# Weight casts of more than 512 columns, issued as two casts of 512

## The chip, the cores and the metric

The kernel runs on one core of a Trainium2 chip. A core has several engines that run side by side, each through a queue of its own: TensorE (PE in the profile; its weight loads are PEld), VectorE (DVE), ScalarE (ACT), GpSimd (POOL), and SyncE (SP), which here issues the transfers. The metric is the device time of one execution in microseconds (us).

## The reference

The reference is a decoder trunk of two layers over 512 tokens with 1024 features, in float32. Each layer adds to the residual stream half of a SwiGLU feed-forward block, then a mixer, then half of a second feed-forward block, each behind an RMS norm; the first mixer is a chunked gated linear attention, the second a stick-breaking attention. A final RMS norm ends it.

```python
def swiglu(h, w_gate, w_up, w_down):
    return (jax.nn.silu(h @ w_gate) * (h @ w_up)) @ w_down
...
for i in range(DEPTH):
    x = x + 0.5 * swiglu(rmsnorm(x, ffn1_norm[i]), ffn1_w_gate[i], ffn1_w_up[i], ffn1_w_down[i])
    h = rmsnorm(x, mix_norm[i])
    ...
    x = x + y.astype(x.dtype)
    x = x + 0.5 * swiglu(rmsnorm(x, ffn2_norm[i]), ffn2_w_gate[i], ffn2_w_up[i], ffn2_w_down[i])
return rmsnorm(x, final_norm)
```

The hidden width of a feed-forward block is 2816, so the four blocks hold most of the weights and of the products.

## The kernel before, in words

Activations lie feature by feature: eight tiles of 128 features by 512 tokens. Every float32 operand of a large product is split into a high part, which is the value cast to the type that TensorE takes (F32R), and a low part, which is the value minus the high part. A product of two such operands is three products on TensorE: high by high, low by high, high by low.

For the weights this split is made on the chip. A `Chunk` is one transfer of weights into a raw tile; an `Entry` is a step of work, which consists of one to four weight units and a body that issues TensorE's products. `Entry.split` takes each unit, casts it on ScalarE into the high tile `wh` (L138) and subtracts on VectorE to get the low tile `wl` (L139). Most units are 128 partitions by 1024 columns; some are 512. Where a unit comes as a tuple of two pieces, each piece of 512 columns has its own cast and subtraction. The large `wh` and `wl` tiles rotate through four buffers each, so a cast must wait until TensorE has finished with the unit that had its buffer before; units of fewer than 1024 columns have one buffer.

`Feed` holds the entries in the order of the program. `Feed.start` issues the splits of up to three entries ahead (at most four large units), the views of four and the transfers of six, and then starts the entry's body. So the casts for a later entry are written ahead of the products and evacuations of the present one. Within each engine the order of the queue is laid out when the program is built, from the written order and from what would be ready; TensorE's order in most of the feed-forward phases is the written one, by `tc.issue_after(st["pe"])`.

Most of the gate and up products and a third of the down products use a scheme of seven block products in place of eight (`FFN.seven`, `seven_down`). Its weight units are a quarter of the weights, sums of quarters that VectorE makes (`sums_12`, L694 and L695; `sums_34`, L700 and L701; L368 to L376 for the down weights), and the other quarters. Each sum tile is written by two VectorE instructions of 512 columns. The seven products run as body_1 and body_2:

```python
prod(w, a11, 0, half(0, 0))
nc.scalar.copy(z, w)
yield
prod(q, s, 0, lambda j: self.t_half(0, j))
nc.scalar.copy(pair(o1[:, H:T]), flat(q))
yield
prod(w, s, 4, lambda j: self.t_half(1, j), first=False)
```

`nc.scalar.copy(z, w)` is L736: ScalarE copies the first accumulator `ps_w` into `ps_z`, after which the third product adds to `ps_w`. The products are L709. ScalarE also evacuates accumulators (L739, L742, L754) and applies the gate's activation (L719); VectorE adds (L722, L755, L759). `seven_down` has the same pattern (products L384, copy L402, additions L390).

The first three entries are split by hand in `begin` and do not pass through L138.

Of the kernel before, what the change touches and what calls it, by code (L numbers as in the profile page):

```python
# [46 lines left out]
def decoder(ctx: ExitStack, tc: tile.TileContext, a: dict, out: bass.AP):  # L47
    nc = tc.nc
# [59 lines left out]
    class Entry:  # L108
# [13 lines left out]
        def split(self):  # L122
            if self.W is None:
                self.W = []
                for r, (_, _, n, m) in zip(self.view(), self.units):
                    few = n * m < 1024
                    if few:

                        h, l = (
                            st["few"].tile([P, n * m], F32R, tag="v" + t, bufs=1, name="w" + t) for t in "hl"  # L130
                        )
                    else:
                        h, l = (wp.tile([P, n * m], F32R, tag="w" + t, bufs=4, name="w" + t) for t in "hl")
                    h, l = (t.rearrange("p (n m) -> p n m", m=m) for t in (h, l))
                    pieces = r if isinstance(r, tuple) else (r,)
                    for i, part in enumerate(pieces):
                        k = slice(i * n // len(pieces), (i + 1) * n // len(pieces))
                        st["cut"] = nc.scalar.copy(h[:, k], part).ins  # L138
                        nc.vector.tensor_tensor(out=l[:, k], in0=part, in1=h[:, k].bitcast(F32), op=ALU.subtract)  # L139
                    self.W.append((h, l))  # L140

# [335 lines left out]
    st = {}  # L477
# [1427 lines left out]
```

## Time and profile before

| what | value |
|---|---|
| time, median of 3 runs (lowest to highest) | 1781.22 us (1780.61 to 1783.96) |
| span of the profiled execution | 1780.3 us |
| PE, PEld busy | 1760.9, 1632.9 us |
| DVE busy | 1538.8 us |
| ACT busy | 1050.4 us, 1830 instructions |
| transfers | 179.24 MB, 101 GB/s in the mean |

The profiled execution is given by its span, from the first to the last instruction; the page shows no time around it. The engine rows give the time in which an engine ran at least one instruction, with the share of the span and the number of instructions. A group of instructions is written as line, engine, operation, output tile and input tile, shapes and count; after the bar come its busy time and the mean duration of one in ns, then the idle time of the engine just before such instructions and what ended it. A wait is written as engine, waiting tile and line, `<-`, engine, tile and line of what released it, then us in total, number of times and, in most rows, the longest. The chain is the work that ended last, followed back from the end: each piece has its start, its length and what ran. The mean granted clock of TensorE was 0.999 of full speed.

### The profile page before, as it was taken

How to read it: one execution, taken by the hardware profiler on the slowest of the kernel's cores; microseconds unless marked ns; L12 is line 12 of the kernel's file. 1: busy time of each engine (PE TensorE's matmuls, PEld its weight loads, DVE VectorE, ACT ScalarE, POOL GpSimd, SP SyncE). 2: the span in 40 equal slices, each digit the busy share in tenths (PEclk: the TensorE clock that was granted, in tenths of full speed). 3: DMA queues.
4: the chain of work that ended last, by engine and by line, in shares of the span. 5: the costliest groups of instructions: out<-in, count | busy, mean ns of one | idle time of the engine just before them, and what ended most of it. 6: DMA issues, size and time to landing. Idle time of an engine off the chain costs nothing.

```text
span 1780.3 us, 31182 instructions
## 1 busy us (share of the span) xinstructions
PE 1760.9 (99%) x12714; PEld 1632.9 (92%) x12714; DVE 1538.8 (86%) x2527; ACT 1050.4 (59%) x1830; POOL 9.8 (1%) x24
## 2 busy tenths in 40 slices
PE   9999999999999999999999999999999999999998
PEld 8999999889888899999889999999888888999997
DVE  8999797786878999889798988977898679998986
ACT  7556455554655556555555555655888755565554
POOL 0000000100000000000000000000000000000000
PEclk9999999999999999999999999999999999999999
DMA  5433334322122333333323233322212233333331
GB/s 167 142 115 112 107 97 131 93 72 72 49 95 95 106 108 119 107 107 108 114 88 119 96 119 104 122 84 83 83 48 72 71 95 119 111 103 111 104 125 53
DMA packets 178755, 179.24 MB, mean 101 GB/s; under 512 B 4082, under 2 KB 170276, under 8 KB 178612
## 3 DMA queue, kind: packets, MB, share of 16 engines
q1 hardware_dynamic: 177760, 175.91, 31.5%
q8 instruction: 99, 1.62, 0.4%
q0 software_dynamic: 608, 1.05, 0.2%
q14 instruction: 44, 0.36, 0.1%
q10 hardware_dynamic: 244, 0.29, 0.0%
HBM read 175.17 MB, written 2.10 MB: 100 GB/s over the span
## 4 chain that ended last, share of the span: by engine, by line
PE 62%; DVE 26%; ACT 7%; issue 3%; DMA 1%; DVEq 0%; ACTq 0%; SPq 0%
PE ps_w L709 13%; PE ps_d L80 12%; PE ps_f L80 8%; DVE wl L139 8%; PE ps_q L709 6%; PE ps_t L80 5%; PE ps_z L709 3%; PE ps_b L80 3%; ACT wh L138 3%; PE ps_w L384 2%; DVE x L390 2%; PE ps_z L1394 1%; DVE ts L816 1%; DVE xn L800 1%; DVE nl L807 1%
## 5 line engine op out<-in xcount | busy, mean ns | idle before, releaser
L139 DVE TENSOR_TENSOR wl<-raw,wh 128x1024 fp32r<-128x1024 f32 x241 | 254.9, 1058 | 58.4 <-ACT wh L138 57.7
L138 ACT CAST wh<-raw 128x1024 fp32r<-128x1024 f32 x241 | 221.7, 920 | 72.7 <-PE ps_f L80 21.6
L139 DVE TENSOR_TENSOR wl<-s,wh 128x1024 fp32r<-128x1024 f32 x176 | 214.3, 1218 | 42.2 <-ACT wh L138 41.9
L138 ACT CAST wh<-s 128x1024 fp32r<-128x1024 f32 x176 | 184.3, 1047 | 102.1 <-DVE s L701 25.7
L709 PE MATMUL ps_w<-th,wh 128*128 128x256 f32 x864 | 239.9, 278 | 4.5 <-ACT ps_z L736 3.4
L709 PE MATMUL ps_w<-tl,wh 128*128 128x256 f32 x864 | 237.7, 275 | 0.0
L709 PE MATMUL ps_w<-th,wl 128*128 128x256 f32 x864 | 237.7, 275 | 0.0
L709 PEld LDWEIGHTS ps_w<-th,wh 128*128 128x128 f32 x864 | 165.8, 192 | 8.2 <-ACT ps_z L736 7.9
L80 PE MATMUL ps_f<-xh,wh 128*128 128x512 f32 x432 | 166.1, 385 | 1.1 <-DVE x L260 1.1
L709 PEld LDWEIGHTS ps_w<-tl,wh 128*128 128x128 f32 x864 | 165.9, 192 | 0.0
L709 PEld LDWEIGHTS ps_w<-th,wl 128*128 128x128 f32 x864 | 165.9, 192 | 0.0
L80 PE MATMUL ps_f<-xh,wl 128*128 128x512 f32 x432 | 164.2, 380 | 0.5 <-DVE wl L139 0.5
L80 PE MATMUL ps_f<-xl,wh 128*128 128x512 f32 x432 | 164.0, 380 | 0.0
L80 PE MATMUL ps_d<-hl,wh 128*128 128x512 f32 x416 | 158.0, 380 | 0.9 <-DVE hl L807 0.8
L80 PE MATMUL ps_d<-hh,wh 128*128 128x512 f32 x416 | 157.7, 380 | 0.2 <-ACT hh L806 0.2
L80 PE MATMUL ps_d<-hh,wl 128*128 128x512 f32 x416 | 157.7, 379 | 0.0
L138 ACT CAST wh<-rawd 128x1024 fp32r<-128x1024 f32 (+1 forms) x100 | 82.7, 844 | 61.2 <-PE ps_d L80 44.5
L139 DVE TENSOR_TENSOR wl<-rawd,wh 128x1024 fp32r<-128x1024 f32 (+1 forms) x100 | 95.9, 962 | 15.3 <-ACT wh L138 15.2
L80 PEld LDWEIGHTS ps_f<-xh,wh 128*128 128x128 f32 x432 | 81.7, 189 | 12.5 <-DVE x L260 1.5
L80 PEld LDWEIGHTS ps_f<-xl,wh 128*128 128x128 f32 x432 | 81.7, 189 | 11.5
L80 PEld LDWEIGHTS ps_f<-xh,wl 128*128 128x128 f32 x432 | 81.7, 189 | 11.4 <-DVE wl L139 0.9
L339 DVE SCALAR_TENSOR_TENSOR x<-ps_d,x 128x512 f32<-128x512 f32 x120 | 79.9, 682 | 13.7 <-PE ps_d L80 13.5
(352 smaller groups left out, 5245.8 us busy)
## 6 DMA issues: line engine op xcount, KB each, us to landing
raw<-in_ffn_w_gate_dram SPq DMA_DIRECT2D x43, 1024.0 KB, 5.4
raw<-in_ffn_w_up_dram SPq DMA_DIRECT2D x43, 1024.0 KB, 5.4
rawd<-in_ffn_w_down_dram SPq DMA_DIRECT2D x84, 512.0 KB, 3.7
raw<-in_gla_w_in_dram SPq DMA_DIRECT2D x12, 1024.0 KB, 5.3
raw<-in_sb_w_in_dram SPq DMA_DIRECT2D x16, 512.0 KB, 3.7
raw<-in_gla_w_out_dram SPq DMA_DIRECT2D x4, 1024.0 KB, 5.0
raw<-in_sb_w_in_dram SPq DMA_DIRECT2D x4, 1024.0 KB, 5.1
raw<-in_sb_w_out_dram SPq DMA_DIRECT2D x4, 1024.0 KB, 4.9
```

Of the source, the lines that this page charges most:

```text
L80: st["pe"] = nc.tensor.matmul(ps, l, r, start=first, stop=last).ins
L138: st["cut"] = nc.scalar.copy(h[:, k], part).ins
L139: nc.vector.tensor_tensor(out=l[:, k], in0=part, in1=h[:, k].bitcast(F32), op=ALU.subtract)
L339: nc.vector.scalar_tensor_tensor(out=x, in0=flat(ps), scalar=0.5, in1=x, op0=ALU.mult, op1=ALU.add)
L384: st["pe"] = nc.tensor.matmul(ps, l_, r_, start=first and c + n == 0, stop=c == 1 and n == 2, skip_group_check=True).ins
L390: nc.vector.scalar_tensor_tensor(out=x, in0=ps, scalar=0.5, in1=x, op0=ALU.mult, op1=ALU.add)
L709: st["pe"] = nc.tensor.matmul(o, l_, r_, start=first and j + n == 0, stop=j == 3 and n == 2, skip_group_check=True).ins
L800: nc.vector.scalar_tensor_tensor(out=t, in0=xs[k], scalar=g, in1=st["R"], op0=ALU.mult, op1=ALU.mult)
L807: nc.vector.tensor_tensor(out=l, in0=t, in1=h.bitcast(F32), op=ALU.subtract)
L816: nc.vector.tensor_tensor(out=o, in0=p, in1=q, op=ALU.subtract)
L1394: nc.tensor.matmul(o_, l_, r_, start=first, stop=last, skip_group_check=True)
```

## The change

The cast of a piece at L138 is issued in steps of `512 // m` rows of the unit, where `m` is the length of a row. A unit of 8 x 128, 4 x 256 or 2 x 512 columns gets two casts of 512 columns; a piece of 512 columns or fewer still gets one. The subtraction stays one instruction over the whole piece. The result of the cast is no longer kept in `st["cut"]`.

```diff
                         k = slice(i * n // len(pieces), (i + 1) * n // len(pieces))
-                        st["cut"] = nc.scalar.copy(h[:, k], part).ins
+                        rows = k.stop - k.start
+                        step = max(1, min(rows, 512 // m))
+                        for a0 in range(0, rows, step):
+                            nc.scalar.copy(h[:, k.start + a0 : k.start + a0 + step], part[:, a0 : a0 + step])
                         nc.vector.tensor_tensor(out=l[:, k], in0=part, in1=h[:, k].bitcast(F32), op=ALU.subtract)
```

## The prediction

> **What bounds the kernel now.** I read the page's sums first, then its chain, then the busy time by stage, and then the waits that end at the operations around the casts.
>
> ```profile
> span 1780.3 us, 31182 instructions
> PE 1760.9 (99%) x12714; PEld 1632.9 (92%) x12714; DVE 1538.8 (86%) x2527; ACT 1050.4 (59%) x1830; POOL 9.8 (1%) x24
> ...
> PE 62%; DVE 26%; ACT 7%; issue 3%; DMA 1%; DVEq 0%; ACTq 0%; SPq 0%
> ```
>
> TensorE is busy for 99% of the span, so no more than 1780.3 - 1760.9 = 19.4 us of it are open gaps. The chain all the same leaves TensorE for 38% of its length: VectorE and ScalarE run beside it with hardly any spare time, and the chain changes over to them wherever TensorE waited a little. The sums by stage show where:
>
> ```profile
> 20.00:70.00 50.00, 49.43 (x250) 42.37 (x249) 49.32 (x79) 28.20 (x45) 0.00 (x0) 1.00 0.37 117
> 100.00:150.00 50.00, 49.86 (x422) 48.84 (x422) 47.72 (x81) 28.37 (x51) 0.00 (x0) 1.00 0.31 96
> 1550.00:1600.00 50.00, 49.77 (x441) 49.29 (x441) 49.27 (x81) 30.85 (x58) 0.00 (x0) 1.00 0.34 106
> 1600.00:1650.00 50.00, 49.95 (x381) 47.83 (x380) 41.55 (x69) 25.98 (x46) 0.00 (x0) 1.00 0.37 116
> ```
>
> After the length of the stretch come the busy times of PE, PEld, DVE and ACT. In the feed-forward phases VectorE is busy for 41.6 to 49.3 of 50 us while TensorE never falls under 49.4; ScalarE stays at 26 to 31. ScalarE is not short of time, but it works strictly in its queue's order, and some of what it does is waited for at once. One piece of the chain, from just before a TensorE gap, shows that:
>
> ```profile
> 150.50 0.35 DVE o L755
> 150.85 0.02 issue
> 150.87 0.42 ACT o L719
> 151.29 0.94 ACT wh L138
> 152.22 0.58 ACT o L719 x2
> 152.81 0.94 ACT wh L138
> 153.75 0.28 ACT ps_z L736
> 154.03 0.04 issue
> 154.07 1.60 PE ps_w L709 x12
> ```
>
> Two whole casts (L138) stand in ScalarE's queue between the gate (L719) and the copy of one accumulator into another (L736), and TensorE's next product waits for that copy. The waits in total:
>
> ```profile
> PEld ps_w L709 <- ACT ps_z L736: 7.9, 18, 1.4
> DVE wl L139 <- ACT wh L138: 114.8, 93, 6.5
> ACT wh L138 <- DVE s L701: 25.7, 4, 7.6
> ACT wh L138 <- DVE s L695: 20.6, 15, 4.7
> ACT o L719 <- DVE o L755: 46.9, 32, 2.9
> ```
>
> So the weight loads waited 18 times for such a copy, 7.9 us together, and VectorE waited 93 times for a cast, 114.8 us together.
>
> **What changes, and how many.** Every cast of L138 over 512 columns becomes two of 512; the subtraction behind it (L139) stays one instruction and now waits for the second half. The groups of that line, by shape:
>
> ```profile
> L138 ACT CAST wh<-s 128x1024 fp32r<-128x1024 f32 x176 | 184.3, 1047 | 102.1 <-DVE s L701 25.7 <-DVE s L695 20.6 <-PE ps_d L80 16.7
> L138 ACT CAST wh<-raw 128x1024 fp32r<-128x1024 f32 x169 | 176.9, 1047 | 71.6 <-PE ps_f L80 21.6 <-PE ps_b L80 16.8 <-PE ps_q L709 8.3
> L138 ACT CAST wh<-rawd 128x1024 fp32r<-128x1024 f32 x52 | 54.5, 1047 | 61.2 <-PE ps_d L80 44.5 <-issue 7.5 <-DMA rawd<-in_ffn_w_down_dram 4.9
> L138 ACT CAST wh<-raw 128x512 fp32r<-128x512 f32 x72 | 44.8, 622 | 1.2 <-DMA raw<-in_ffn_w_gate_dram 1.2
> ```
>
> 176 + 169 + 52 = 397 casts are cut, so ScalarE runs 1830 + 397 = 2227 instructions. The 512-column casts that exist already stay as they are. No transfer is added or moved, nothing changes on SP's, POOL's or TensorE's queue, and the assignment that goes with the old cast (`st["cut"]`) is read nowhere, so dropping it costs nothing.
>
> **The price of one cut.** Whole durations say 2 x 622 - 1047 = 197 ns. But ScalarE's records overlap. The kernel has pairs of 512-column casts today, where a unit comes in two pieces:
>
> ```profile
> 165.36 1.15 ACT L138 CAST wh<-rawd 128x512 fp32r<-128x512 f32 x2
> 166.43 0.39 ACT L719 ACTIVATE o<-ps_z 128x256 f32<-128x256 f32 x1
> ...
> 169.77 1.03 ACT L138 CAST wh<-s 128x1024 fp32r<-128x1024 f32 x1
> 170.70 0.41 ACT L719 ACTIVATE o<-o 128x256 f32<-128x256 f32 x1
> ```
>
> The pair is done after 1.15 us, the single cast after 1.03 (1.05 in the mean): 0.10 to 0.12. The next instruction starts 1.07 after the pair's start and 0.93 after the single's: 0.14, part of which may belong to the next one. I take 0.105 us, nearest to the group's mean (1.15 - 1.047), and keep 0.10 and 0.14 as bounds; the 197 ns belong to halves that do not run back to back and serve as the far end. ScalarE then works 397 x 0.105 = 42 us more, some 61% of the span; over the whole kernel that has room.
>
> **What of it lies on the path.** By the sums of the chain's list:
>
> ```profile
> by line: PE ps_w L709 13.4%; PE ps_d L80 12.5%; PE ps_f L80 7.7%; DVE wl L139 7.6%; PE ps_q L709 6.3%; PE ps_t L80 4.9%; issue 3.2%; PE ps_z L709 3.2%; PE ps_b L80 3.0%; ACT wh L138 2.6%; PE ps_w L384 2.1%; DVE x L390 1.9%; PE ps_z L1394 1.
> ...
> 21.43 1.07 ACT wh L138
> ...
> 1702.21 0.94 ACT wh L138
> ```
>
> 2.6% of 1780.3 us are 46.3 us of casts. At 0.94 us each, the piece that the chain shows for a whole cast, this is 49 casts. A few pieces of that sum are 512-column casts, which do not change, or casts of which the chain holds only a part; counted in the list from 21.43 us to 1702.21 us, 38 pieces are 0.93 us or longer. If the order of the queues stays, a path that is one connected chain grows by at least what is added on it: 38 x 0.105 = 4.0 us as the lower end, 49 x 0.105 = 5.1 us as the other, 49 x 0.14 = 6.9 us with the dearer price. Off the chain a cast lies beside TensorE's products: its buffer was freed a few products earlier, and 0.1 us is covered. Where that cover is gone, it would show as more waits of VectorE for casts, 93 x 0.105 = 9.8 us at most. Nothing is gained by the subtraction or the products: both wait for the whole unit as before (a product with the high part is followed at once by one with the low part).
>
> The one place with a possible gain are the 176 casts of sums. A sum tile is written by two VectorE instructions, and the first half of the cast needs only the first of them:
>
> ```profile
> L701 DVE TENSOR_TENSOR s<-raw,s 128x512 f32<-128x512 f32 x72 | 49.1, 681 | 0.0
> ```
>
> So the first half can run beside the second of those 0.68 us instructions, and the cast ends some 0.4 us earlier (1.05 less 0.62). But ScalarE waited for L695 and L701 only 19 times, and the chain passes to the casts mostly from the gates, as above. From below nothing, from above 19 x 0.4 = 7.6 us if each of them bound; I take 0.5 us, near the lower end, since the waits for L755 on the path are not touched by it.
>
> The sum: 1780.3 + 5.1 - 0.5 = 1784.9 us for the span of this execution, a ratio of 1.0026. The page gives nothing around the span; it lies 0.9 us under the median of the runs, 1781.22. On the median this is 1785.8, and I write 1786.
>
> **A rule against the row.** The Trainium skill, Advanced Engine Details and Errata, section The Read-Write Bubble, advises tiles of 512 or 1024 elements alike to keep the bubble between ScalarE's instructions small. By that rule the cut would matter little, the path would grow by about nothing, and the time would stay at 1781. The rows disagree with treating both alike: 622 ns for 512 columns are 1.21 ns a column, 1047 ns for 1024 are 1.02.
>
> **The rivals.** First, the order stays and the path grows, as summed: 1784 to 1789, likeliest 1786. Second, the cost is hidden: VectorE's work at 98% of some stages sets the pace, a late copy only uses up time in which TensorE would have waited for VectorE a little later. For it speaks the DVE share of 26% in the chain, against it that the chain runs through ScalarE in between without a break. Time: 1781. The skill's rule above ends here too.
>
> Third, on the other side: ScalarE's queue is laid out anew when the program is built, and with halves as units a copy or gate can be put between them. In the piece shown the copy would start half a cast, 0.53 us, earlier, more than the mean wait of 7.9 / 18 = 0.44 us, so its wait would vanish. Each such case also saves the two times 0.105 us of its casts. Against the 5.1 us of the sum this decides from about 8 of the 18 cases on (8 x 0.65 = 5.2); with all 18 it gives 5.1 - 11.7 = -6.6 us, with most of them 1776. Against it: the cast stood ahead of the copy in the queue because it was written earlier and was ready, and that holds for its second half as well.
>
> Fourth, the new layout goes the wrong way: gates or subtractions fall behind halves in stages where VectorE has no spare time (49.3 of 50). The price: 93 waits of VectorE for a cast, each 0.105 longer, are 9.8 us on top of 5.1: 1796.
>
> **How the numbers follow.** A change under 0.2% (3.6 us) is about what a measurement of this kernel cannot tell from none. First case 0.46, of which 0.06 fall under 1784.8; hidden 0.17; halves taken apart to advantage 0.25; worse layout 0.12. So faster 0.25, same 0.17 + 0.06 = 0.23, slower 0.40 + 0.12 = 0.52. The range takes in the hidden case, the middle of the gain and most of the worse layout: 1776 to 1795. The likeliest case's own range is 1784 to 1789.
>
> **What would show it.** In the changed profile: 794 more casts of 512 columns and none of 1024 on the cast's line; pairs of 1.15 us; ScalarE busy by 42 us more (78 if the halves stand apart); the weight loads' wait for the copy of L736 up from 7.9 us by some 0.2 us a case; VectorE's wait for casts up from 114.8 us. Wrong would be: halves with a copy or gate between them and a smaller wait for L736 (third case), or an unchanged wait of TensorE (second), or VectorE's waits for casts up by more than 10 us (fourth).

## The result and the profile after

| | median | lowest to highest | runs |
|---|---|---|---|
| before | 1781.2 us | 1780.55 to 1783.96 | 15 |
| after | 1785.12 us | 1784.1 to 1786.81 | 15 |

The ratio is 1.0020, with a 95% interval of 1.0014 to 1.0027: 3.9 us more, a small but clear loss. The profiled execution of the changed kernel took 1784.56 us for a span of 1782.6, so 2.0 us lie around a span. The profile of before, with its span of 1780.3, thus came from an execution in the upper part of its runs, and the two spans differ by only 2.3 us where the medians differ by 3.9.

From the page of the changed kernel, the sums, the shares of the chain by engine, and the casts by shape (the copy's line is now L141, the subtraction L142, and all later lines are three further down):

```profile
span 1782.6 us, 31599 instructions
PE 1761.3 (99%) x12714; PEld 1632.3 (92%) x12714; DVE 1540.3 (86%) x2527; ACT 1084.8 (61%) x2227; POOL 9.9 (1%) x24
...
PE 60%; DVE 28%; ACT 7%; issue 4%; DMA 1%; DVEq 0%; SPq 0%; ACTq 0%
...
L141 ACT CAST wh<-raw 128x512 fp32r<-128x512 f32 x410 | 238.6, 620 | 69.3 <-PE ps_f L80 20.3
L141 ACT CAST wh<-s 128x512 fp32r<-128x512 f32 x352 | 202.1, 617 | 121.9 <-DVE s L697 38.3
...
L141 ACT CAST wh<-rawd 128x512 fp32r<-128x512 f32 x152 | 88.0, 619 | 57.8 <-PE ps_d L80 27.1
```

410 + 352 + 152 = 914 casts of 512 columns, 794 more than before, and none of 1024. ScalarE is busy for 1084.8 us, 34.4 more: 87 ns a cut. TensorE and VectorE do the same work as before.

The same piece of the chain as in the prediction, and the waits that answer to those shown there:

```profile
150.34 0.35 DVE o L758
150.68 0.02 issue
150.71 0.42 ACT o L722
151.12 1.03 ACT wh L141 x2
152.15 0.59 ACT o L722 x2
152.74 1.02 ACT wh L141 x2
153.76 0.28 ACT ps_z L739
154.04 0.04 issue
154.09 1.60 PE ps_w L712 x12
```

```profile
PEld ps_w L712 <- ACT ps_z L739: 10.5, 20, 1.5
DVE wl L142 <- ACT wh L141: 117.0, 93, 6.6
ACT wh L141 <- DVE s L697: 38.3, 16, 3.3
```

Each cast of the piece holds the chain for 1.03 us where it held it for 0.94, and the copy behind the two comes that much later. The weight loads' waits for the copy grew by 2.6 us, VectorE's waits for casts by 2.2 us.

### The profile page after: what moved, and what is told of

It is laid out like the page before. It is cut to its first block, busy times and chain, and to the rows that moved or that the text cites. A ratio compares the mean times of both kernels' runs of the same rounds, so it can differ in the third digit from the quotient of the medians.

```text
span 1782.6 us, 31599 instructions
## 1 busy us (share of the span) xinstructions
PE 1761.3 (99%) x12714; PEld 1632.3 (92%) x12714; DVE 1540.3 (86%) x2527; ACT 1084.8 (61%) x2227; POOL 9.9 (1%) x24
## 4 chain that ended last, share of the span: by engine, by line
PE 60%; DVE 28%; ACT 7%; issue 4%; DMA 1%; DVEq 0%; SPq 0%; ACTq 0%
PE ps_w L712 13%; PE ps_d L80 12%; DVE wl L142 8%; PE ps_f L80 8%; PE ps_q L712 6%; PE ps_t L80 4%; PE ps_b L80 3%; PE ps_z L712 3%; ACT wh L141 3%; PE ps_w L387 2%; DVE x L393 2%; DVE s L697 1%; DVE ts L819 1%; DVE xn L803 1%; DVE s L704 1%
## 5 line engine op out<-in xcount | busy, mean ns | idle before, releaser
L142 DVE TENSOR_TENSOR wl<-raw,wh 128x1024 fp32r<-128x1024 f32 x241 | 255.2, 1060 | 59.2 <-ACT wh L141 56.8
L141 ACT CAST wh<-raw 128x512 fp32r<-128x512 f32 x410 | 238.6, 620 | 69.3 <-PE ps_f L80 20.3
L141 ACT CAST wh<-s 128x512 fp32r<-128x512 f32 x352 | 202.1, 617 | 121.9 <-DVE s L697 38.3
L142 DVE TENSOR_TENSOR wl<-s,wh 128x1024 fp32r<-128x1024 f32 x176 | 214.7, 1220 | 44.8 <-ACT wh L141 44.5
L712 PEld LDWEIGHTS ps_w<-th,wh 128*128 128x128 f32 x864 | 165.8, 192 | 10.5 <-ACT ps_z L739 10.5
L141 ACT CAST wh<-rawd 128x512 fp32r<-128x512 f32 x152 | 88.0, 619 | 57.8 <-PE ps_d L80 27.1
L142 DVE TENSOR_TENSOR wl<-rawd,wh 128x1024 fp32r<-128x1024 f32 (+1 forms) x100 | 95.9, 962 | 15.7 <-ACT wh L141 15.6
```

The lines of the kernel that those rows point to most:

```text
L141: nc.scalar.copy(h[:, k.start + a0 : k.start + a0 + step], part[:, a0 : a0 + step])
L712: st["pe"] = nc.tensor.matmul(o, l_, r_, start=first and j + n == 0, stop=j == 3 and n == 2, skip_group_check=True).ins
```

## The experiments

The changed kernel differs from the one before in two ways: the casts are cut, and the queues are laid out anew, since the layout is made from the instructions that there are. In the changed kernel's queue 48 of the 397 cut casts have something between their halves, in 11 places the copy of L736 into `ps_z` (only one of these is among the 18 copies that the weight loads waited for before); some 200 places of ScalarE's queue and 270 of VectorE's hold another instruction. Four theories were set against each other. A: the price of the cut, some 0.1 us, lies on the path. B: the cut is hidden, and the new layout costs the time. C: VectorE sets the pace, and a wait taken from TensorE comes back elsewhere. D: each cut costs the same wherever it stands.

To hold a layout fixed, the kernels below end with an edge between each instruction and the next of the same engine in a given list; an edge orders the queue and is meant to add no wait:

```diff
+        for a_, b_ in zip(flat_, flat_[1:]):
+            tc.add_manual_dep(b_, a_.name, info, reason="pinned order")
```

**Old order, cut casts, and new order, whole casts.** In the first, the casts are cut as in the change and the two halves stand side by side in the order of before. In the second, the casts are those of before, in the order of the changed kernel.

> All casts cut in two, but every engine's queue is held in the order of the kernel before, the two halves side by side. Theory A (the price of the cut itself, about 0.1 us a cast, lies on the path): 1781.2 + 4 = 1785 us, like the changed kernel. Theory B (the cut is hidden, and the new layout of the queues costs the time): 1781 us. Halfway, 1783, would mean both.

> The casts are whole again, but every engine's queue is held in the order of the changed kernel; a whole cast stands where the second half stood (where the first half stood in the 3 cases in which another wide cast lies between). Theory A: 1781 us, the time of before. Theory B: 1785 us, the time of the changed kernel.

| kernel | median | ratio to before, interval |
|---|---|---|
| old order, halves | 1785.16 us | 1.0027 (1.0016 to 1.0038) |
| new order, whole | 1781.28 us | 1.0002 (0.9992 to 1.0011) |

Before took 1780.25 us beside them. The cut alone costs 4.9 us (2.8 to 6.8), the layout alone nothing that can be measured: theory B falls. No run holds the kernel before in its own order, but the second of the two has edges as well and takes the time of before, so the edges cost nothing that can be measured either. The waits of the first of the two are those of the changed kernel:

```profile
PEld ps_w L735 <- ACT ps_z L762: 10.6, 19, 1.5
```

**Quarters.** The step is 256 columns in place of 512, in the old order:

```diff
-                        step = max(1, min(rows, 512 // m))
+                        step = max(1, min(rows, 256 // m))
```

> Casts in steps of 256 columns in the order of the kernel before: a cast of 1024 columns becomes four, one of 512 becomes two. Theory A: each wide cast costs three cuts and not one, so 1781.2 + 3 x 4 = 1793 us, and 1 to 2 us more where the narrow casts lie on the path too. Theory B: as far as the cuts stay hidden, 1781 to 1783 us.

The step is at least one row of the unit, so the 28 wide casts of units of 2 x 512 columns still became two and not four; the other 369 became four, and 120 narrow ones two. ScalarE ran 3085 instructions, 1255 more than before.

It took 1800.02 us, ratio 1.0110 (1.0096 to 1.0124): 19.8 us more, well over the 13 to 14 that theory A gave by multiplying, and over the 15.5 that 1255 cuts give at the 4.9 us of 397. The chain's list of this kernel shows why the product was too small (first its share by lines, then the same piece as above):

```profile
by line: PE ps_d L101 10.0%; PE ps_w L735 9.9%; DVE wl L165 9.7%; PE ps_f L101 7.4%; ACT wh L162 6.3%; PE ps_q L735 4.6%; PE ps_t L101 4.6%; issue 3.4%; PE ps_b L101 2.8%; PE ps_z L735 2.5%; DVE x L416 2.0%; PE ps_w L410 1.9%; DVE hl L833 1
...
152.88 1.21 ACT wh L162 x4
154.09 0.59 ACT o L745 x2
154.68 1.21 ACT wh L162 x4
155.89 0.28 ACT ps_z L762
```

A cast holds the chain for 1.21 us, so each cut more still costs (1.21 - 0.94) / 3 = 0.09 us. But casts now make up 6.3% of 1797.9 us on the chain, 113 us or 94 casts' worth at 1.21, where it was 49 before, and the subtractions behind them (`wl`) 9.7% in place of 7.6: the path has moved onto ScalarE and VectorE in more places. The price of one cut stays, the number of cuts that count grows.

**Cuts on the chain and off it.** In the old order, only those casts are cut that the chain's list of before holds, 51 by their start times, or only the 346 others:

```diff
-                        step = max(1, min(rows, 512 // m))
+                        st["casts"] = st.get("casts", -1) + 1
+                        step = max(1, min(rows, 512 // m)) if st["casts"] in ON_PATH else rows
```

> In the order of the kernel before, only the 51 wide casts that stand on its chain are cut (those of the chain's list, matched by their start times). Theory A (what is added on the chain is added to the time): 51 x 0.09 = 4.6 us, so about 1785 us, as with all 397. Theory D (each cut costs the same wherever it stands): 51 / 397 of 4.9 us, 0.6 us, 1781 us.

> In the order of the kernel before, only the other 346 wide casts are cut. Theory A: 1781 us, at most 1 to 2 us more where a cast off the chain is short of 0.1 us. Theory D: 346 / 397 of 4.9 us, 4.3 us, 1785 us.

| kernel | median | ratio to before, interval | more than before, per cut |
|---|---|---|---|
| 51 on the chain | 1783.60 us | 1.0016 (1.0007 to 1.0025) | 3.0 us (1.2 to 4.5), 59 ns |
| 346 off it | 1782.93 us | 1.0013 (1.0004 to 1.0022) | 2.3 us (0.7 to 3.9), 7 ns |

Before took 1780.59 us beside them. Theory D falls: it gave 0.6 and 4.3 us, both outside the intervals. Theory A gave 4.6 us for the 51, at the edge of the interval, and nothing or at most 1 to 2 us for the 346. A cast on the chain costs eight to nine times as much as one off it by the medians, but the 346 together cost nearly half, so the chain is not all. Their sum, 5.3 us, is near the 4.9 of all cuts together. The weight loads' waits for the copy, first in the kernel with the 51, then in the one with the 346:

```profile
PEld ps_w L738 <- ACT ps_z L765: 9.2, 17, 1.6
```

```profile
PEld ps_w L738 <- ACT ps_z L765: 8.1, 20, 1.3
```

Before, they were 7.9 us in 18 waits. With the 51 they grew by 1.3 us; with the 346 by 0.2, so these casts cost most of their 2.3 us at other places, which no run here picks out.

**The copy ahead of the cast.** Whole casts in the old order, but the 18 copies (L736) that the weight loads waited for stand one place earlier in ScalarE's queue:

```diff
 gate, cast, gate, gate,
-cast, copy
+copy, cast
```

> Whole casts and the order of the kernel before, except that the 18 copies into ps_z that the weight loads waited for (7.9 us in all) stand one place earlier, ahead of the wide cast before them. Theory A (these waits are on the path): up to 7.9 us less, 1774 to 1778 us, and no weight load waits for those copies. Theory C (VectorE sets the pace, and TensorE only waits a little later instead): the waits for the copy go, the time stays at 1781 us.

It took 1778.41 us beside 1780.25, ratio 0.9989 (0.9980 to 0.9997). In place of 18 waits and 7.9 us there were 2 waits and 0.7 us, and 1.8 us came out of it. What grew in the down product:

```profile
PEld ps_w L405 <- DVE x L411: 4.0, 14, 0.3
PEld ps_w L405 <- ACT ps_z L423: 2.5, 8, 0.4
```

Before, these two were 1.9 us in 8 waits and 0.2 us in 1. The down product's steps now wait longer for VectorE's additions and for copies of their own, 4.4 us more together. So a further kernel moved those 16 pairs of copies ahead of their wide cast too:

> Whole casts, the 18 copies (L736) ahead of the wide cast before them as in the run with the copy first, and the 16 pairs of copies of the down product (L402) moved ahead of their wide cast as well, for which the weight loads waited 2.5 us once the first waits were gone. If those waits are on the path: 1 to 2 us less than with the 18 alone, 1776 to 1777 us. If VectorE's lateness only shows in another wait: 1778 us.

It took 1780.59 us, ratio 1.0000 (0.9991 to 1.0009): no gain over before was left. A piece of its chain and its longest wait of a weight load:

```profile
133.11 0.33 ACT ps_z L423
133.44 0.98 ACT wh L159
134.42 0.02 issue
134.45 1.23 DVE wl L160
135.67 0.60 DVE hl L828
136.27 1.01 DVE x L411 x3
137.28 0.04 issue
137.33 1.60 PE ps_w L405 x12
```

```profile
PEld ps_w L405 <- DVE x L411: 10.0, 16, 0.8
```

With the copies in front, the cast comes later; VectorE's subtraction waits for it and stands ahead of the additions, for which the weight loads now wait 10.0 us, against 4.0 with the 18 alone. This is theory C at work: a place in ScalarE's queue is paid for in VectorE's.

**The copy between the halves.** All casts cut, and the 18 copies between the two halves of the cast that they stood behind, which is what cutting could at best be good for:

> All casts cut, in the order of the kernel before, but the 18 copies into ps_z that the weight loads waited for stand between the two halves of the wide cast that they stood behind. Theory A: the price of the cuts stays (4.9 us), the copies start half a cast earlier and their waits (10.6 us with the halves) mostly go, which was worth 1.8 us where whole casts were moved behind the copy: 1783 to 1784 us. The forecast's third case priced each of these at 0.65 us and would give 1774 to 1776 us.

It took 1784.81 us, ratio 1.0023 (1.0013 to 1.0033), against 1.0027 with the halves side by side: no difference that these intervals can tell. The waits for these copies went from 10.6 to 1.6 us, and the down product waited longer instead:

```profile
PEld ps_w L408 <- ACT ps_z L426: 5.2, 13, 0.6
PEld ps_w L408 <- DVE x L414: 3.7, 12, 0.3
...
PEld ps_w L733 <- ACT ps_z L760: 1.6, 4, 1.0
```

With the halves side by side the down product's weight loads had waited 1.1 us for the additions (L414 here), and the profile lists no wait for the copies (L426 here).

**The cast ahead of the late gate.** In the prediction's piece ScalarE stands idle for 1.87 us before the first gate, which waits for VectorE:

```profile
150.87 0.42 ACT L719 ACTIVATE o<-o 128x256 f32<-128x256 f32 x1 [1.87 <-DVE o L755]
```

The cast behind that gate could run in this time. Here the cast goes first and the copy keeps its new place, in 16 of the 18 places:

```diff
-gate, cast, gate, gate, cast, copy
+cast, gate, gate, gate, copy, cast
```

> Whole casts; in 16 of the 18 places the order on ScalarE goes from gate, cast, gate, gate, cast, copy to cast, gate, gate, gate, copy, cast, so that the first cast fills the time in which ScalarE waits for VectorE before its gate; in the other 2 only the copy goes ahead of the cast. Everything else as in the kernel before. Theory A: the copy's waits go as with the copy first (1778.4 us), and the subtractions get their casts earlier, so 1775 to 1778 us. If the gates, now later, are waited for, or VectorE sets the pace anyway: 1778 to 1780 us.

> The same order with all casts cut in two. Theory A: 26 of the 51 casts that stood on the chain are taken off the path to the copy, so the cut costs less here than the 4.9 us that it costs in the old order: 2 to 3 us more than the same order with whole casts. If the price has nothing to do with that path: 5 us more.

| kernel | median | ratio to before, interval |
|---|---|---|
| whole casts | 1777.02 us | 0.9979 (0.9970 to 0.9988) |
| all casts cut | 1780.52 us | 0.9999 (0.9990 to 1.0008) |

Before took 1780.71 us beside them. The whole casts in this order beat both kernels of this study, by 3.7 us against the one before. This is both moves together: the copy's alone gave 1.8 us, and the 1.9 us that the cast's move adds is not clear of the intervals. In the piece, the cast now starts at 149.56 us where it started at 151.19. The waits below are of the kernel with whole casts. Before, the gates had waited 46.9 us in 32 cases for the same addition, and the subtractions 114.8 us for casts:

```profile
ACT o L740 <- DVE o L776: 17.9, 17, 1.5
DVE wl L160 <- ACT wh L159: 110.4, 90, 6.5
```

A part of the gates' waits only moved on: for the addition after that one (L759 before) they now wait 10.8 us in 27 cases, against 4.3 in 12.

The cut costs 3.5 us here against 4.9 in the old order. The medians lie between the two expectations, 2 to 3 us and 5, and the intervals are too wide to tell 3.5 from either. Whether taking casts off the chain makes the cut cheaper stays open.

## Why the prediction was right

The forecast was 1786 us and slower, 4.6 us over before; 1785.12 was measured, 3.9 over before (2.5 to 4.8). The 0.9 us by which the forecast went from span to median is not the time around a span, which is 2.0 us; since only the difference to before counts, nothing hangs on it.

**The price of one cut** was taken as 0.105 us from the pair in the trace. On the chain it is 0.09 (1.03 less 0.94), and ScalarE's busy time rose by 87 ns a cut, 34 us in place of 42. The 197 ns from whole durations were rightly put aside: the records overlap.

**How many count.** The sum took 49 casts on the chain at the full price, 5.1 us, and nothing for the others. The total was near (4.9 us in the fixed order), but its two parts were both off. The casts on the chain brought 3.0 us (1.2 to 4.5), 59 ns each and not 105. The lower end of the sum, the 38 pieces of 0.93 us or longer, comes to 3.4 us at the measured 0.09; it is the better reading, since the 49 count as whole casts pieces that the chain holds only in part. What is left between 3.4 and 3.0 is within the interval. The casts off the chain, costed at nothing behind TensorE's products, brought 2.3 us (0.7 to 3.9): at 7 ns of 90 each, most of their price was covered, as said, but not all. That the two errors nearly cancel was luck.

**The place** was right: the copy (L736) behind two casts and the gates. Its waits rose from 7.9 to 10.5 us; 0.2 us for each of 18 cases would have been 3.6. VectorE's waits for casts rose by 2.2 us, far from the 9.8 named as the most. That holds for the casts on the chain; where the others cost their part is not shown.

**The early half of a sum's cast** was given 0.5 us. In the old order with halves, where only the cut differs, the casts' wait of 20.6 us in 15 cases for the second of the two sums (L695) became two waits, 12.8 us in 8 cases together, the first of them for the first sum:

```profile
ACT wh L162 <- DVE s L720: 9.9, 3, 3.5
ACT wh L162 <- DVE s L721: 2.9, 5, 0.7
```

So first halves do start earlier. In the changed kernel's own layout they wait longer, 38.3 us in 16 cases for the first of the two sums (L697) alone. No run sets the early start apart from the rest of the cut, and whether it was worth anything stays open.

**The rivals.** Hidden cost: refuted, the cut alone costs 4.9 us. The worse layout: refuted, the new layout with whole casts takes the time of before. The halves taken apart: the new layout does put a copy between halves in 11 places, but only one of them is among the 18 late copies that the forecast priced, so the case did not come about; and the price that it gave, 0.65 us for each, was wrong: with all 18 copies placed so by hand the kernel took 4.2 us more than before in place of 4.9, a difference within the intervals, while the down product waited longer.

**The rule on tile sizes.** The Trainium skill, Advanced Engine Details and Errata, section The Read-Write Bubble, advises tiles of 512 or 1024 elements alike. By it the time would have stayed at 1781. The runs disagree for this kernel: 512 columns cost 4.9 us over 1024, and 256 cost 19.8. The direction of the rule, larger tiles, agrees.

## What to carry to other kernels

An instruction cut in two pays its fixed cost on whatever path runs through it, and a queue that has something urgent behind it is such a path even when its engine is busy for only 59% of the time, as ScalarE here. Before cutting work so that urgent work can get in between, look at where the queue waits for nothing useful: in this kernel, moving 16 casts into the idle time ahead of a late gate, together with 18 copies ahead of a cast, gained 3.7 us, and cutting all casts lost 3.9. And a wait removed in one queue is worth what is left after other waits have taken its place: 7.2 us of the weight loads' waits gone were 1.8 us of time.

## What the runs showed of the hardware that had not been expected

Back to back on ScalarE, a cast of 1024 columns takes 0.94 us of the queue, two of 512 take 1.03 and four of 256 take 1.21: 0.09 us for each instruction more, half of the 197 ns that the whole durations suggest. The loss, though, grew by a factor of four from halves to quarters (4.9 to 19.8 us) where the number of cuts grew by a factor of 3.2 (397 to 1255), as more of the chain went over to ScalarE.
